# Modulation rows through GpSimd's queue, and every low part of a weight on VectorE, during the state steps

## The chip, the cores and the metric

The kernel runs on one core of a Trainium2 chip. The metric is the time of one execution on the device in microseconds (us); three runs of the kernel before are at hand, and one more execution was profiled.

Names of the engines in the rows: PE is TensorE (PEld its loading of weights), DVE is VectorE, ACT is ScalarE, POOL is GpSimd, SP is SyncE, which here only issues transfers. A name with q at its end (SPq, POOLq) is the engine's sequencer, which waits and issues.

## The reference

One layer of a streaming encoder on 512 frames (`SEQ`) of width D = 2048, in float32: a mixer and a feed-forward part, each between two normalisations. A conditioning vector `c` gives shift, scale and gate for both.

```python
mod = jax.nn.silu(c) @ ada_w + ada_b
...
sh_m, sc_m, g_m, sh_f, sc_f, g_f = jnp.split((mod + ada_table[layer])[:, None, :], N_MOD, axis=-1)
h = _rms(x, norm_mix_pre[layer]) * (1 + sc_m) + sh_m
...
x = x + g_m * _rms(y, norm_mix_post[layer])
h = _rms(x, norm_ffn_pre[layer]) * (1 + sc_f) + sh_f
f = _conv_ffn(h, ffn_w_in[layer], ffn_conv_w[layer], ffn_conv_b[layer], ffn_w_out[layer])
x = x + g_f * _rms(f, norm_ffn_post[layer])
```

The mixer is RWKV-7 with 32 heads of 64. For each head a 64 x 64 state goes through the frames:

```python
sa = jnp.einsum("bhvk,bhk->bhv", state, a_t)
state = (state * w_t[:, :, None, :] + sa[..., None] * b_t[:, :, None, :]
         + v_t[..., None] * k_t[:, :, None, :])
return state, jnp.einsum("bhvk,bhk->bhv", state, r_t)
```

`r`, `k` and `v` are products of the mixed input with 2048 x 2048 weights; the result is normalised per head, gated and multiplied by `w_o`.

## The kernel before

Tiles are 128 channels by 512 frames, so there are KT = 16 blocks of channels (two heads each). Every large product is made in three passes (`mm3`, lines 266 to 273): the 128 x 128 weight and the moving tile are each split into a high part, which is the value rounded to TensorE's faster float32 form, and a low part, the rest; high x high, high x low and low x high are added up in one bank of PSUM.

The weights lie in HBM in the order of their use (`plan`). `w_load` brings a chunk of eight 128 x 128 blocks by SP's queue into one of three buffers `wr`. `w_split` makes the high part `wh` of half a chunk (four blocks, 128 x 512) on ScalarE (line 225) and the low part `wl` by a subtraction (line 227). Which engine subtracts is set by `wst["pool"]`: 0 is VectorE always, 1 is GpSimd always, 2 is GpSimd for every other half. It is 1 in the first stage, 0 from then on, 2 from the start of the state steps (set in `begin`), and 0 again at the output product. Splits run two halves ahead of their use, in four buffers each.

The state is computed in chunks of 64 frames, for two heads at a time, in KT = 16 state steps p = 0 to 15 of eight chunks each. For each step small matrices come through HBM (`d_gs`, `d_bnd`, `d_e`, `d_kp`, `d_vt`), loaded by SP. `inverse(n)` inverts 32 x 32 triangular blocks for four steps at once, in 31 pairs of short GpSimd instructions (lines 715 and 717), after 16 small loads `ia` (line 705), and its result is stored and read back as `tn` and `tt`. `solve(p)` builds a step's matrices (its last products are line 793, which need `tt` as VectorE has filled it in at lines 786 and 787), `transfer` its products (lines 826 and 845), `chain` carries the state on (lines 868 and 876), and `norm` makes the output `y`, which goes by GpSimd's queue to `d_y` (line 908) and comes back by SP as `rl` until there is room for it on the chip. Meanwhile TensorE multiplies the `r` weights, block by block.

All of this is written as generators in a list `sides`; each `mm3` ends with a `tick()`, which moves every generator one yield on, and a few loops tick without a product while something must be waited for. The order of the instructions on each engine is laid out when the kernel is built, by a planner that starts from the order of the program and works with its own costs (`schedule_with_timeline_sim=True`); each engine and each queue then runs its instructions in that order and waits on semaphores.

Shift, scale and gate of the later parts are 64 blocks of 128 values, each a product of 128 rows of `ada_w` with `silu(c)`. `row_jobs` makes them on VectorE: it loads a block of rows to a tile `js`, multiplies it by the row vector `crow` and sums along the row (line 473), and adds the bias (line 474). It has `bufs` buffers, loads the next block some ticks after a block's product, and goes on to the next block after `pace` ticks. `with behind():` puts the product behind the newest low part that VectorE has made. `scan_rows` does 20 of the 64 blocks during the state steps, in two halves of 1024 columns (so 40 loads of 512 KB), with one buffer.

Of the kernel before, what the change touches and what calls it, by code (L numbers as in the profile page):

```python
# [16 lines left out]
P = 128  # L17
# [17 lines left out]
def row_blocks(d):  # L35

    return [(vi, b) for vi in range(2, 6) for b in range(d // P)]
# [122 lines left out]
def body(ctx, tc, g, ap):  # L160
    nc = tc.nc
    KT, FT, GT, D = g.KT, g.FT, g.GT, g.D
    V, S, G, PE = nc.vector, nc.scalar, nc.gpsimd, nc.tensor
# [41 lines left out]
    wst = {"load": 0, "split": 0, "use": 0, "raw": {}, "half": {}, "pool": 0, "end": g.mid}  # L205
# [57 lines left out]
    def behind(on=True):  # L263

        return tc.issue_after(wst["last"].ins) if on else nullcontext()
# [181 lines left out]
    ROWS = row_blocks(D)  # L447
# [4 lines left out]
    def c_row(t, cols=slice(0, D)):  # L452

        n = cols.stop - cols.start
        nc.sync.dma_start(t, d_c.rearrange("k p -> (k p)")[cols].unsqueeze(0).to_broadcast([P, n]))
        return t

    def row_jobs(todo, crow, get, bufs, pace, cols=slice(0, D), lag=0):

        got = {}  # L460

        def load(i):
            if i < len(todo):
                got[i] = get(i % bufs)
                nc.sync.dma_start(got[i], ap["ada3"][ROWS.index(todo[i])][:, cols])

        for i in range(bufs):
            load(i)
        yield
        for n, (vi, b) in enumerate(todo):  # L470
            w, to = got.pop(n), part[:, b:b + 1]
            with behind():
                V.scalar_tensor_tensor(w, w, 1.0, crow, ALU.mult, ALU.mult, accum_out=to)  # L473
            V.tensor_tensor(mods[vi][:, b:b + 1], to, mods[vi][:, b:b + 1] if cols.start else bt[:, vi, b:b + 1], ALU.add)
            for _ in range(lag):
                yield
            load(n + bufs)
            for _ in range(pace - lag):
                yield
# [31 lines left out]
    nc.sync.dma_start(d_c.rearrange("k p -> p k"), cs)  # L511
    crow = c_row(vp.tile([P, D], F32, name="crow"))
    jobs = row_jobs([r for r in ROWS if r[0] == 4], crow, lambda i: vp.tile([P, D], F32, tag="js", name="js", bufs=2), 2, 9)
    vouts = [v_out(vbank[j], j) for j in range(nv0)]
    for o in vouts:
# [54 lines left out]
    def c2(tag, bufs=1, shape=(P, NC, HD)):  # L570
        return pool_of[0].tile(list(shape), F32, tag=tag, name=tag, bufs=bufs)
# [153 lines left out]
    def load_a(p):  # L725
        n, q = p // BP, p % BP
        rhs, ab, tn = (sc.tile([P, NC, n], F32, tag=t, name=t) for t, n in (("rhs", P), ("ab", 32), ("tn", 32)))
        for i, hv in enumerate(HV):
            nc.sync.dma_start(rhs[hv], d_gs[p][hv, :, HD * i:HD * i + P])
            o = 2 * HD * (1 - i)  # L730
            nc.sync.dma_start(ab[i * HD + 32:i * HD + 64], d_gs[p][i * HD + 32:i * HD + 64, :, o:o + 32])
        for h in range(2):
            nc.sync.dma_start(tn[h * HD:h * HD + 32], d_tn[n][q, h, 0].rearrange("c i j -> i c j"))
            for d in range(2):
                o = h * HD + d * 32
                nc.sync.dma_start(TT[o:o + 32, :, o:o + 32], d_tt[n][q, h, d].rearrange("c i j -> i c j"))
        return rhs, ab, tn

    def load_b(p):
        for i, hv in enumerate(HV):  # L740
            nc.sync.dma_start(BH[hv, :, HD - i * HD:P - i * HD], d_bnd[p][hv, :, 2 * i])
        E = sc.tile([P, NC, HD], F32, tag="E", name="E")
        nc.sync.dma_start(E, d_e[p])
        return E

    def load_k(p):
        kp = c2("kp")
        nc.sync.dma_start(kp, d_kp[p])
        return kp

    def load_v(p, h):
        t = svs[h] = c2(f"sv{h}", 1, (P, NC // 2, 2, HD))
        vt = d_vt[p][h * T // 2:(h + 1) * T // 2].rearrange("(c t) (h i) -> h t c i", t=HD, i=HD)
        nc.sync.dma_start(t[HD:P, :, 0], vt[0])
        nc.sync.dma_start(t[0:HD, :, 1], vt[1])
        if h == 0:
            V.memset(t[0:HD, 0, 0], 0.0)
            V.memset(t[HD:P, 0, 1], 0.0)
# [9 lines left out]
    def solve(p):  # L768

        rhs, ab, tn = ld_a.pop(p)  # L770
        up = bank(3, (P, NC, 32))
        us = ab
        for c in range(NC):
            for h in range(2):
                lo = slice(h * HD + 32, h * HD + 64)
                PE.matmul(up[h * HD:h * HD + 32, c], ab[lo, c], TT[lo, c, lo], start=True, stop=True)
        S.copy(us[0:32], up[0:32])
        S.copy(us[64:96], up[64:96])
        for _ in range(2):
            yield  # L780
        wz = bank(3, (P, NC, 32))
        for c in range(NC):
            for h in range(2):
                hi = slice(h * HD, h * HD + 32)
                PE.matmul(wz[hi, c], tn[hi, c], us[hi, c], start=True, stop=True)
        V.tensor_copy(TT[0:32, :, 32:64], wz[0:32])
        V.tensor_copy(TT[64:96, :, 96:128], wz[64:96])
        for _ in range(2):
            yield
        for c0 in (0, 4):  # L790
            hb = bank(4 if c0 else 3, (P, 4, P))
            for c in range(c0, c0 + 4):
                PE.matmul(hb[:, c - c0], TT[:, c], rhs[:, c], start=True, stop=True)  # L793
            cp_ = V.tensor_copy if c0 else S.copy
            cp_(LH[0][HV[1], c0:c0 + 4], hb[HV[1]])
            cp_(LH[1][HV[0], c0:c0 + 4], hb[HV[0]])
            yield
        if p + 1 < KT:
            ld_a[p + 1] = load_a(p + 1)
# [122 lines left out]
    def invert_ready(done):  # L922
        for n in range(NB):
            if n not in begun and done >= (n + 1) * BP:
                begun.add(n)
                sides.append(inv[n])
# [55 lines left out]
    def scan_rows():  # L982
        for cols in (slice(0, D // 2), slice(D // 2, D)):
            row = c_row(c2("crow", 1, (P, D // 2)), cols)
            yield from row_jobs(ROWS[:KT + KT // 4], row, lambda i: c2("js", 1, (P, D // 2)), 1, 8, cols, 2)

    def begin():
        while fixed in sides or inv[0] in sides:
            yield
        ld_a[0], ld_b[0] = load_a(0), load_b(0)  # L990
        for i, hv in enumerate(HV):
            nc.sync.dma_start(LH[i][hv, :, HD - i * HD:P - i * HD], d_bnd[0][hv, :, 2 - 2 * i])
        while s1_last in sides:
            yield
        invert_ready(KT)
        ss_stack.close()
        pool_of[0] = ss_stack.enter_context(tc.tile_pool(name="scn2", bufs=1))
        opened.append(True)
        wst["pool"] = 2
        ld_k[0] = load_k(0)  # L1000
        yield from solve(0)
        load_v(0, 0)
        load_v(0, 1)
        jobs.append(scan_rows())
        sides.extend((s2_a, s2_b, jobs[0]))

    sides.append(begin())
    for b in range(KT):
        ps = bank((kb[KT % 3], kb[(KT - 2) % 3])[b] if b < 2 else 0)
# [141 lines left out]
    for b in range(KT - NL):  # L1151
        if b >= KT - NL - 4:
            fetch_x(*divmod(b - (KT - NL - 4), 2))
        ps = po[b] if b < n0 else kinner("wo", b, yx, bank((2, 6)[b % 2]))
        block_out(b, ps, acc1, yo[b], sqs[b % 2])
        if b == 1:
            jobs = row_jobs(ROWS[KT + KT // 4:2 * KT], c_row(spare("b2", "crow", D)),
                            lambda i: tp.tile([P, D], F32, tag=f"t3{'hl'[i]}", name="js"), 2, 8)
            sides.append(jobs)
# [398 lines left out]
```

## Time and profile before

| | us |
|---|---|
| median of 3 runs | 2728.54 (2727.55 to 2728.64) |
| profiled execution | 2731.33 |
| its span, first to last instruction | 2729.5 |
| TensorE busy | 2573.4 (94%) |
| VectorE busy | 2041.8 (75%) |
| ScalarE busy | 1329.7 (49%) |
| GpSimd busy | 610.8 (22%) |

The profiled execution took 2.8 us more than the median. Busy time of TensorE is modelled, since its products are pipelined: what shows whether it sets the time is where it stands idle and what ended the idle time, and the clock that was granted to it, since at half the clock a product takes twice as long. Idle time of another engine costs nothing by itself.

### The profile page before, as it was taken

Reading aid. Unit: us, or ns where it says so; the run is one execution under the profiler, and the core shown is the slowest. Engines: PE = TensorE matmul, PEld = TensorE weight load, DVE = VectorE, ACT = ScalarE, POOL = GpSimd, SP = SyncE. Lnnn points to the kernel's source line nnn. Section 1 sums busy time; section 2 is a strip of 40 time slices with the busy share of each in tenths; the row PEclk is TensorE's granted clock in tenths of the full one; section 3 lists DMA queues with packets and bytes.
Section 4 is the critical chain, followed back from the end, with each engine's and each line's share of the span. In section 5 each row is a group of like instructions: output and inputs, shape, how many; then the busy total and the mean of one; then the engine's idle time right before and its main releaser. Section 6 shows DMA issues by size and latency. Waiting matters only on the chain.

```text
span 2729.5 us, 46869 instructions
## 1 busy us (share of the span) xinstructions
PE 2573.4 (94%) x17630; PEld 2253.4 (83%) x17630; DVE 2041.8 (75%) x3225; ACT 1329.7 (49%) x2313; POOL 610.8 (22%) x722
## 2 busy tenths in 40 slices
PE   5899999988999998999889999999999999999997
PEld 3568877767778776788789999999999987788896
DVE  6978678887776777667898888888878876544477
ACT  4442355544345445435665555555555553243464
POOL 3543114667531110001422112121121100000000
PEclk8999999999999999999999999999999999999998
DMA  8759876656776666386567767777677658523366
GB/s 304 278 185 388 294 225 209 202 209 208 206 213 179 187 186 169 118 321 219 178 198 205 201 187 198 196 195 204 189 200 197 168 209 287 192 93 101 98 203 205
DMA packets 282419, 559.73 MB, mean 205 GB/s; under 512 B 124016, under 2 KB 157168, under 8 KB 274256
## 3 DMA queue, kind: packets, MB, share of 16 engines
q1 hardware_dynamic: 252400, 445.24, 50.9%
q0 software_dynamic: 29360, 110.77, 15.2%
q8 instruction: 139, 2.28, 0.3%
q14 instruction: 88, 0.72, 0.1%
q10 hardware_dynamic: 432, 0.72, 0.1%
HBM read 478.38 MB, written 78.26 MB: 204 GB/s over the span
## 4 chain that ended last, share of the span: by engine, by line
PE 57%; DMA 10%; DVE 5%; issue 2%; ACT 1%; POOL 1%; SPq 1%; DVEq 0%; ACTq 0%; POOLq 0%
PE bk L1338 10%; PE bk L1336 10%; PE bk L1337 10%; PE bk L270 7%; PE bk L272 7%; PE bk L271 7%; DMA js<-ada 4%; PE bk L845 2%; DMA act<-d_act 1%; DMA tt<-d_tt 1%; PE bk L876 1%; PE bk L793 1%; DVE wl L227 1%; DVE js L473 1%; DMA wr<-w 1%
## 5 line engine op out<-in xcount | busy, mean ns | idle before, releaser
L270 PE MATMUL bk<-xh,wh 128*128 128x512 f32 (+1 forms) x2204 | 781.8, 365 | 23.5 <-ACT wh L225 6.1
L272 PE MATMUL bk<-xh,wl 128*128 128x512 f32 (+1 forms) x2204 | 764.1, 362 | 26.7 <-DVE wl L227 22.6
L271 PE MATMUL bk<-xl,wh 128*128 128x512 f32 (+1 forms) x2204 | 783.9, 360 | 2.1 <-DVE xl L1140 1.7
L225 ACT CAST wh<-wr 128x512 fp32r<-128x512 f32 x584 | 358.0, 620 | 532.9 <-PE bk L271 438.7
L227 DVE TENSOR_TENSOR wl<-wr,wh 128x512 fp32r<-128x512 f32 x518 | 368.9, 717 | 238.3 <-ACT wh L225 221.5
L270 PEld LDWEIGHTS bk<-xh,wh 128*128 128x128 f32 x2204 | 419.7, 192 | 87.9 <-ACT wh L225 7.4
L272 PEld LDWEIGHTS bk<-xh,wl 128*128 128x128 f32 x2204 | 409.4, 191 | 98.8 <-DVE wl L227 33.6
L271 PEld LDWEIGHTS bk<-xl,wh 128*128 128x128 f32 x2204 | 421.3, 192 | 63.1 <-DVE xl L1140 2.7
L1338 PE MATMUL bk<-xh,wl 128*128 128x256 f32 x832 | 235.7, 283 | 0.1
L1336 PE MATMUL bk<-xh,wh 128*128 128x256 f32 x832 | 235.4, 283 | 0.0
L1337 PE MATMUL bk<-xl,wh 128*128 128x256 f32 x832 | 235.4, 283 | 0.0
L1287 POOL DMA_DIRECT2D ss<-w x78 | 68.0, 871 | 623.6 <-DMA ss<-w 385.7
L473 DVE SCALAR_TENSOR_TENSOR js<-js,crow 128x1024 f32<-128x1024 f32 (+1 forms) x100 | 153.8, 1540 | 59.0 <-DMA js<-ada 53.5
L227 POOL TENSOR_TENSOR wl<-wr,wh 128x512 fp32r<-128x512 f32 x66 | 97.7, 1484 | 295.1 <-ACT wh L225 280.1
L1338 PEld LDWEIGHTS bk<-xh,wl 128*128 128x128 f32 x832 | 159.7, 192 | 0.5 <-DVE wl L1323 0.5
L1337 PEld LDWEIGHTS bk<-xl,wh 128*128 128x128 f32 x832 | 159.7, 192 | 0.0
L1336 PEld LDWEIGHTS bk<-xh,wh 128*128 128x128 f32 x832 | 159.7, 192 | 0.0
L1338 PE MATMUL bk<-xh,wx 128*128 128x256 f32 x416 | 117.7, 283 | 0.0
L1336 PE MATMUL bk<-xh,wx 128*128 128x256 f32 x416 | 117.7, 283 | 0.0
L1337 PE MATMUL bk<-xl,wx 128*128 128x256 f32 x416 | 117.7, 283 | 0.0
L1440 POOL TENSOR_TENSOR fo<-fo,rs 128x256 f32<-128x256 f32 x4 | 3.6, 911 | 494.0 <-ACT rs L1102 494.0
L1481 DVE TENSOR_TENSOR xl<-act,xh 128x512 fp32r<-128x512 f32 (+1 forms) x172 | 92.2, 552 | 26.1 <-ACT xh L1480 26.1
(290 smaller groups left out, 5658.2 us busy)
## 6 DMA issues: line engine op xcount, KB each, us to landing
wr<-w SPq DMA_DIRECT2D x370, 512.0 KB
ss<-w SPq DMA_DIRECT2D x78, 512.0 KB
ss<-w POOLq DMA_DIRECT2D x78, 512.0 KB, 8.5
js<-ada SPq DMA_DIRECT2D x72, 512.0 KB
ada<-ada SPq DMA_DIRECT2D x32, 1024.0 KB
js<-ada SPq DMA_DIRECT2D x28, 1024.0 KB
w<-w SPq DMA_DIRECT2D x39, 512.0 KB
d_bnd<-bnd POOLq DMA_DIRECT2D x16, 768.0 KB, 3.7
```

The source lines that it names most:

```text
L225: S.copy(hi, r)
L227: ins = on.tensor_tensor(lo, r, hi.bitcast(F32), ALU.subtract)
L270: PE.matmul(out[:, cs], wh[0:kp, 0:m], xh[0:kp, cs], start=start, stop=False)
L271: PE.matmul(out[:, cs], wh[0:kp, 0:m], xl[0:kp, cs], start=False, stop=False)
L272: PE.matmul(out[:, cs], wl[0:kp, 0:m], xh[0:kp, cs], start=False, stop=stop)
L473: V.scalar_tensor_tensor(w, w, 1.0, crow, ALU.mult, ALU.mult, accum_out=to)
L845: PE.matmul(qb[:, c], LH[i][:, 4 * h + c], RH[i][:, :, 4 * h + c], start=True, stop=True)
L1287: G.dma_start(t[:, i], chunk(j, other), accum_op=ALU.add)
L1336: PE.matmul(ps, wh, xh, start=start and k == 0, stop=False, skip_group_check=True)
L1337: PE.matmul(ps, wh, xl, start=False, stop=False, skip_group_check=True)
L1338: PE.matmul(ps, wl, xh, start=False, stop=k == CH - 1, skip_group_check=True)
L1481: V.tensor_tensor(ahl[e][1][:, cs], act[f][:, cs], ahl[e][0][:, cs].bitcast(F32), ALU.subtract)
```

## The change

The rows of the state steps are loaded by GpSimd's queue (`G` is `nc.gpsimd`) in place of SP's; the other users of `row_jobs` keep SP's. And `wst["pool"]` is no longer set to 2 in `begin`, so it stays 0 and VectorE makes every low part from there on.

```diff
-    def row_jobs(todo, crow, get, bufs, pace, cols=slice(0, D), lag=0):
+    def row_jobs(todo, crow, get, bufs, pace, cols=slice(0, D), lag=0, q=nc.sync):
 
         got = {}
 
         def load(i):
             if i < len(todo):
                 got[i] = get(i % bufs)
-                nc.sync.dma_start(got[i], ap["ada3"][ROWS.index(todo[i])][:, cols])
+                q.dma_start(got[i], ap["ada3"][ROWS.index(todo[i])][:, cols])
...
-            yield from row_jobs(ROWS[:KT + KT // 4], row, lambda i: c2("js", 1, (P, D // 2)), 1, 8, cols, 2)
+            yield from row_jobs(ROWS[:KT + KT // 4], row, lambda i: c2("js", 1, (P, D // 2)), 1, 8, cols, 2, G)
...
         opened.append(True)
-        wst["pool"] = 2
         ld_k[0] = load_k(0)
```

## Rows read from the trace of the kernel before

**Rows 1.** Busy time by stretch: length, then each engine, granted clock, DMA share, GB/s.

```profile
640.00:680.00 40.00, 35.71 (x265) 29.74 (x263) 31.70 (x41) 10.63 (x19) 34.51 (x51) 0.96 0.64 186
680.00:770.00 90.00, 80.80 (x628) 64.95 (x629) 64.84 (x114) 34.81 (x68) 57.19 (x78) 0.92 0.78 208
770.00:1020.00 250.00, 247.95 (x2182) 198.39 (x2181) 179.34 (x347) 120.22 (x233) 32.69 (x30) 1.00 0.71 190
```

**Rows 2.** Instructions of line 227, 680 to 1130 us: minimum, median, maximum in ns.

```profile
L227 DVE TENSOR_TENSOR wl<-wr,wh x34: 673/692/984, 691.0 to 1124.4; 128x512 fp32r<-128x512 f32 x34
...
L227 POOL TENSOR_TENSOR wl<-wr,wh x31: 1257/1277/2279, 692.5 to 1094.3; 128x512 fp32r<-128x512 f32 x31
```

**Rows 3.** List of waits, 680 to 1130 us: in total, times, longest.

```profile
DVE js L473 <- DMA js<-ada: 22.4, 8, 6.8
...
DVE wl L227 <- ACT wh L225: 15.9, 9, 2.6
...
PEld bk L272 <- POOL wl L227: 4.2, 2, 3.8
```

**Rows 4.** Timeline of TensorE's products: start, length, in brackets idle time before.

```profile
725.70 0.79 PE L272 MATMUL bk<-xh,wl 128*128 128x512 f32 x1 [3.41 <-POOL wl L227]
...
734.19 2.05 PE L793 MATMUL bk<-rhs,tt 128*128 128x128 f32 x16
```

**Rows 5.** Busy time by stretch, in the two stretches at half clock.

```profile
725.00:731.80 6.80, 6.10 (x14) 4.79 (x15) 6.35 (x11) 0.62 (x1) 6.41 (x8) 0.50 0.60 174
...
766.00:769.40 3.40, 3.40 (x15) 3.01 (x14) 3.31 (x6) 1.78 (x3) 2.02 (x3) 0.50 0.67 249
```

**Rows 6.** Timeline of GpSimd, the low part that TensorE waited for.

```profile
724.38 1.26 POOL L227 TENSOR_TENSOR wl<-wr,wh 128x512 fp32r<-128x512 f32 x1
```

**Rows 7.** Timeline of VectorE, 708 to 731 us.

```profile
715.22 1.30 DVE L473 SCALAR_TENSOR_TENSOR js<-js,crow 128x1024 f32<-128x1024 f32 x1 [6.77 <-DMA js<-ada]
...
725.23 1.50 DVE L473 SCALAR_TENSOR_TENSOR js<-js,crow 128x1024 f32<-128x1024 f32 x1 [5.20 <-DMA js<-ada]
...
730.40 0.42 DVE L787 COPY tt<-bk 32x256 f32<-32x256 f32 x1
```

**Rows 8.** Timeline of SP's issues, 698 to 748 us.

```profile
698.61 10.90 SPq L705 DMA_DIRECT2D ia<-d_gs x16
...
710.99 0.39 SPq L465 DMA_DIRECT2D js<-ada x1
...
716.56 0.33 SPq L465 DMA_DIRECT2D js<-ada x1
...
747.17 0.56 SPq L465 DMA_DIRECT2D js<-ada x1
```

**Rows 9.** Timeline of VectorE, 741 to 765 us.

```profile
741.03 1.36 DVE L473 SCALAR_TENSOR_TENSOR js<-js,crow 128x1024 f32<-128x1024 f32 x1 [1.30 <-DMA js<-ada]
...
762.92 1.23 DVE L473 SCALAR_TENSOR_TENSOR js<-js,crow 128x1024 f32<-128x1024 f32 x1 [2.79 <-DMA js<-ada]
...
764.49 0.42 DVE L787 COPY tt<-bk 32x256 f32<-32x256 f32 x1
```

**Rows 10.** Timeline of TensorE's products, the stall at 762 us.

```profile
765.01 2.87 PE L793 MATMUL bk<-rhs,tt 128*128 128x128 f32 x16 [2.85 <-issue]
```

**Rows 11.** Instructions of line 227 on GpSimd, 560 to 690 us.

```profile
L227 POOL TENSOR_TENSOR wl<-wr,wh x5: 1265/1402/1745, 636.3 to 675.0; 128x512 fp32r<-128x512 f32 x5
```

**Rows 12.** List of waits of TensorE's products, 636 to 1130 us.

```profile
PE bk L270 <- ACT xh L387: 3.6, 1, 3.6
...
PE bk L686 <- DVE Ab L675: 2.4, 1, 2.4
```

**Rows 13.** Stores of line 908 through GpSimd's queue, 680 to 1130 us.

```profile
L908 POOL DMA_DIRECT2D d_y<-y x14: 540/557/580, 737.0 to 1114.9; - x14
...
DMA to landing us min/median/max: 2.3/4.1/6.0
```

**Rows 14.** Adding loads of line 1287 through GpSimd's queue, 512 KB each.

```profile
DMA to landing us min/median/max: 6.4/8.5/10.4
```

## Prediction

> **What bounds the kernel now.** I read the stage before the engine totals. The state steps lie between about 636 and 1130 us of the span, and the table by stretch [rows 1] is the first view to read there. From 770 to 1020 us TensorE is busy for 247.95 of 250 us and its clock is full; it sets the time, and nothing that VectorE (179.34 busy) or GpSimd (32.69) does there can shorten it. From 680 to 770 it is busy for 80.80 of 90 at a mean clock of 0.92. In that early stretch, and in the short ones at both ends, is all that this change can win or lose directly.
>
> Second, who makes the low parts of the weights (line 227): in 680 to 1130 us VectorE makes 34 at a median of 692 ns, and GpSimd 31 at 1277 ns [rows 2]. Third, the list of waits for the same stretch [rows 3]: TensorE waited for a low part of GpSimd's for 4.2 us in two places, and for none of VectorE's 34. VectorE in its turn stood 22.4 us, eight times, for a row of the modulation (`js`) to land, and 15.9 us for ScalarE's high part in front of its own low parts.
>
> Fourth, the timeline around the longest of these waits. TensorE stands for 3.41 us before the product that takes the low part [rows 4], and the granted clock then is 0.50 (the 1.2 GHz level) from 725.0 to 731.8 us [rows 5]: 6.8 us at half speed, of which TensorE loses 3.4. So this one stall cost 6.8 us. Its low part ran on GpSimd at 724.38 [rows 6], in the middle of the chain of small multiply-adds that inverts the last group of diagonal blocks. VectorE at that time was no better off: it had stood 6.77 us for one row until 715.22, and stood 5.20 us for the next until 725.23; the copy into `tt`, which the product at L793 needs, ended at 730.82 [rows 7]. SP explains the first: it was issuing the 16 small loads of `ia` for 10.90 us from 698.61, so the row's load went out at 710.99; the next went out at 716.56 and landed only after 8.7 us [rows 8].
>
> Fifth, a second stall that rows cause. A `js` load went out at 747.17 [rows 8] although its buffer had been free since 742.39 (741.03 + 1.36 [rows 9]): 4.8 us late on SP. Two products later VectorE stood 2.79 us until 762.92, and the `tt` copies behind that row ended at 764.91 [rows 9]; TensorE, which needs them at L793, stood 2.85 us (the view calls it "issue") until 765.01 [rows 10]. The clock gives way once more for 3.4 us after it [rows 5], 1.7 us lost.
>
> **The change, part by part.** The order of instructions on an engine is laid out when the kernel is built; the trace cannot show the new one, so I leave the old order as it is and move only what the diff moves.
>
> *GpSimd's low parts go to VectorE.* 36 move: the 31 of [rows 2] and five more between 636 and 675 us [rows 11]. GpSimd is rid of the low part that it made late at 724.38. The stall of 3.41 us and the 3.4 us of clock behind it go, if nothing else is late there. What is late next is on VectorE: from 725.70 to L793 at 734.19 [rows 4] are 8.5 us, 3.4 of them lost to the clock, so TensorE, going on at 722.3, would stand at L793 by 727.4, and `tt` would come at 730.82 if the row still lands at 725.23. Then only 734.19 - 730.82 = 3.4 us would be won. But the row loads in front of it can leave earlier: the one of 710.99 waited for SP, and its buffer was free before VectorE fell idle at 708.45 (715.22 - 6.77), 2.5 us before it went out. I take the full **-6.8**, with -3.4 as the other end.
>
> *Their cost on VectorE.* 36 x 0.69 = 24.8 us. In 680 to 1130 it is 31 x 0.69 = 21.4; from 770 to 1020 VectorE has 250 - 179 = 71 us free under a full TensorE, so its share there costs nothing. If that cover were gone it would be 0.69 us per low part. Uncovered are the ends. From 640 to 680 VectorE is busy for 31.70 of 40 [rows 1] and TensorE waits for it (2.4 us for `Ab` [rows 12]): the five are 0 to 3.5 us, taken as **+1**, since the longest of GpSimd's five took 1745 ns against 1265 [rows 11], the two engines were in each other's way, and VectorE gets some of this back. After 1020 us lie 110 of the stretch's 450, so some seven of the 31 if they are evenly spread, among waits of the chain of states: 0 to 5 us, taken as **+1**, for VectorE has free time there too. VectorE also waits in line for ScalarE's high part twice as often; 15.9 us in 34 cases [rows 3] made TensorE wait for no low part, so I charge nothing more.
>
> The row's product (line 473) is put behind the newest low part that VectorE makes, which is now the newest of all; it can only move later, which gives its load more time. Behind it stand `tt`, `qz` and `rh` copies, for which TensorE waits.
>
> *The rows' loads go to GpSimd's queue.* 40 loads of 512 KB leave SP. On SP each took 0.33 to 0.56 us [rows 8] and waited for the row's product; whatever loads stood behind are freed. On GpSimd each stands behind the inversion's steps (57.19 us of work in 78 instructions in 680 to 770, 0.73 us each [rows 1]): about half a step, 0.4 us. While it waits for VectorE's product the inversion waits behind it; that is covered, since the inverted blocks are those of the last four of 16 steps, and the chain is at the first few. Stores of `d_y` wait there too, and are read much later, except at the end. Time to land: on SP 4.2 us (710.99 to 715.22). No load without addition goes by GpSimd's queue in this trace. The nearest rows are the `d_y` stores in these same steps, 256 KB, 2.3 to 6.0 us, median 4.1 [rows 13]; 256 KB more at the stretch's 208 GB/s are 1.3 us, so an estimate of 5.4. The adding loads of 512 KB later in the kernel take 8.5 [rows 14]. I take 5.4, for it is the same queue in the same stretch: 5.4 - 4.2 + 0.4 = 1.6 us more per load. The three loads from 747 to 763 stand in VectorE's way one after another: 3 x 1.6 = 4.8, which is what SP's lateness in front of them gives back. So **0**. The ends: -4.6 if the second stall vanishes (2.85 and the clock's 1.7), and 3 x (8.5 - 4.2 + 0.4) - 4.8 = +9.3 with 8.5 us to land.
>
> *SP's queue is freer.* TensorE waited 3.6 us for a high part of `y` that stood on a fetch through SP near the end of the steps [rows 12]; if the clock fell behind it as behind the first stall, 7.0 in all. The rows are no longer in that queue ahead of it. 0 to -7.0 us; taken as **-1**, since both still share the same transfer engines.
>
> A rule of the Trainium skill speaks against the moved loads. The row: GpSimd's own part of the 14 `d_y` stores took 540 to 580 ns [rows 13], while VectorE was busy for some 72% of the time; it was never held up. The page "SBUF — State Buffer", section "SBUF: two separate sides", states that GpSimd cannot write a DMA's descriptors while VectorE runs an instruction that takes both ports, and that a transfer of about 620 ns then takes about 3100. By the rule each exposed load would be later; by the row, none. The sum goes by the row.
>
> **Sum.** -6.8 + 1 + 1 + 0 - 1 = -5.8 us. The profiled execution took 2731.33 us (span 2729.5), which gives 2725.5; the median of the runs is 2.8 us below it, 2728.54, which gives 2722.7.
>
> **The rivals.** *Stall handed to VectorE (no change).* The low part is made in time, but the rows land as late as now, and TensorE waits for `tt` until 730.82: -3.4 + 1 + 1 - 1 = -2.4, 2726. For it: the row of 725.23 took 8.7 us to land with SP not late at all. Against: SP's 2.5 and 4.8 us of lateness with two others [rows 7 to 9]. Chance 0.30.
>
> *Rows late on GpSimd's queue (slower).* Five loads stand in VectorE's way (those of 715 and 725 us and the three up to 763). With 8.5 us to land each is 4.7 later, 23.5 in all, less SP's 7.3; with -3.4 and +1 for the rest that is +13.8, 2742. It is slower by over 0.2% (5.5 us) from 5x = 5.5 + 3.4 + 7.3 - 1, x = 3.0 us, so from 6.8 us to land. For it: GpSimd works 57 of those 90 us [rows 1]. Against: the 8.5 are of transfers that also read what they add to. Chance 0.20.
>
> *GpSimd held up by VectorE's own instructions (no change).* Each of five exposed loads waits out a row's product, 1.3 to 1.5 us [rows 7]: up to +7.5 on the sum, +1.7, 2730. The 540 to 580 ns speak against it. Chance 0.05. [...]
>
> **How the numbers follow.** Forecast 0.45; the rivals 0.30, 0.20, 0.05. A measurement of this kernel tells about 0.2% (5.5 us) from no change, and the forecast is just beyond. Faster 0.45, same 0.35, slower 0.20. Low end: -6.8 - 4.6 - 7.0 = -18.4, 2710. High end: the slower rival is 2734 at its threshold and 2742 at 8.5 us; I stop at 2740. The forecast's own range is 2710 to 2723.
>
> **What would show it.** No low part on GpSimd after 636 us, 65 on VectorE in the stretch of [rows 2]; no wait of TensorE for a low part; no half clock at 725 to 732; VectorE's wait for rows below 22.4 us, with the first of them, at 715, nearly gone; rows landing in 5 to 6 us; the stretch 770 to 1020 as full as now. I am wrong if TensorE's wait comes back as one for `tt` or `qz` behind a row, if rows take 7 us to land, or if the new order of instructions puts a row's load behind a long part of the inversion.

## The result, and the profile after

The changed kernel takes 2757.4 us (median of four runs, 2752.8 to 2759.84) where the kernel before takes 2728.6: a ratio of 1.0088, 95% interval 1.0068 to 1.0107. It is slower by 0.9%, some 24 us by the ratio and 29 by the medians. The forecast was 2722.7, faster by 5.8 us, with a range that ended at 2740.

The profiled execution took 2758.21 us, 26.9 more than that of before. Busy time by stretch, first of the kernel after (columns as in [rows 1]):

```profile
640.00:680.00 40.00, 35.18 (x255) 30.17 (x254) 33.47 (x45) 10.84 (x20) 36.84 (x52) 0.90 0.62 187
680.00:770.00 90.00, 83.17 (x642) 67.35 (x641) 68.28 (x121) 35.39 (x68) 49.27 (x75) 0.91 0.78 211
770.00:1020.00 250.00, 240.74 (x2029) 190.38 (x2029) 173.53 (x342) 112.11 (x217) 15.51 (x29) 0.97 0.68 176
1020.00:1130.00 110.00, 93.05 (x849) 73.12 (x848) 75.81 (x150) 51.76 (x102) 4.85 (x9) 0.92 0.61 157
1130.00:1420.00 290.00, 265.07 (x1714) 235.38 (x1713) 215.78 (x360) 154.57 (x315) 58.80 (x53) 0.97 0.62 209
```

The two stretches of before that [rows 1] leaves out:

```profile
1020.00:1130.00 110.00, 94.64 (x851) 75.94 (x849) 78.41 (x152) 54.77 (x107) 7.29 (x8) 0.94 0.60 153
1130.00:1420.00 290.00, 267.17 (x1695) 237.42 (x1694) 218.86 (x353) 159.39 (x319) 58.56 (x54) 0.99 0.67 222
```

What TensorE loses in a stretch is its idle time (length less busy) and what the clock takes of the busy time (busy x (1 - clock)). From 680 to 770 us that is 9.2 + 6.5 = 15.7 us before and 6.8 + 7.5 = 14.3 after. From 770 to 1020 it is 2.1 before, and 9.3 + 7.2 = 16.5 after: the stretch that was full is full no longer. With +2.6 (640 to 680), +3.4 (1020 to 1130) and +7.4 (1130 to 1420) the five stretches come to +26.4, nearly all of the 26.9 (an estimate, since the stretches are equal times and not equal work).

The list of waits, 680 to 1130 us, after (in total, times, longest):

```profile
DVE js L473 <- DMA js<-ada: 14.4, 7, 5.3
PE bk L776 <- DMA tt<-d_tt: 10.9, 8, 2.7
PE bk L876 <- DMA sv<-d_vt: 5.6, 5, 2.2
PE bk L826 <- DVE qz L846: 5.4, 2, 3.4
...
PEld bk L272 <- DVE wl L227: 1.1, 1, 1.1
```

and for the same two loads before:

```profile
PE bk L776 <- DMA tt<-d_tt: 5.6, 6, 3.3
...
PE bk L868 <- DMA sv<-d_vt: 1.3, 1, 1.3
PE bk L876 <- DMA sv<-d_vt: 1.1, 1, 1.1
```

VectorE waits less for rows (14.4 us, 22.4 in [rows 3]) and TensorE's wait for a low part is down from 4.2 us to 1.1. What TensorE waits for now are small loads of the state steps on SP's queue: `tt` (32 KB, which `inverse` left in HBM) twice as long, `sv` (64 KB) more than twice; and copies of VectorE's, `qz` above all. The rows land as forecast, here the loads of line 465 through GpSimd's queue (40 of them, ns of issue; the second line is of the landing):

```profile
L465 POOL DMA_DIRECT2D js<-ada x40: 528/528/580, 678.7 to 1168.8; - x40
...
DMA to landing us min/median/max: 4.0/5.6/8.5
```

### The profile page after: what moved, and what is told of

Its sections match the earlier page's. It is cut to its first block, busy times and chain, and to the rows that moved or that the text cites. A ratio compares the mean times of both kernels' runs of the same rounds, so it can differ in the third digit from the quotient of the medians.

```text
span 2756.4 us, 46886 instructions
## 1 busy us (share of the span) xinstructions
PE 2588.9 (94%) x17630; PEld 2264.1 (82%) x17630; DVE 2052.2 (74%) x3261; ACT 1328.4 (48%) x2313; POOL 591.9 (21%) x726
## 4 chain that ended last, share of the span: by engine, by line
PE 60%; DMA 8%; DVE 5%; POOL 2%; issue 2%; SPq 1%; ACT 1%; DVEq 0%; ACTq 0%; POOLq 0%
PE bk L1337 10%; PE bk L1335 10%; PE bk L1336 10%; PE bk L270 8%; PE bk L272 8%; PE bk L271 8%; PE bk L845 2%; DMA wr<-w 1%; DMA js<-ada 1%; PE bk L876 1%; PE bk L793 1%; DVE wl L227 1%; DMA tt<-d_tt 1%; DMA sv<-d_vt 1%; POOL ix L717 1%
## 5 line engine op out<-in xcount | busy, mean ns | idle before, releaser
L227 DVE TENSOR_TENSOR wl<-wr,wh 128x512 fp32r<-128x512 f32 x554 | 392.0, 713 | 255.7 <-ACT wh L225 237.6
L1322 DVE TENSOR_TENSOR wl<-wr,wh 128x512 fp32r<-128x512 f32 x104 | 108.6, 1063 | 3.6 <-ACT wh L1321 1.9
```

The costliest lines, as they stand in the source:

```text
L227: ins = on.tensor_tensor(lo, r, hi.bitcast(F32), ALU.subtract)
L1322: wst["last"] = V.tensor_tensor(lo, r, hi.bitcast(F32), ALU.subtract)
```

## The experiments

Three theories. **A**: the planner lays out a new order of the instructions for the changed kernel, and that order costs the time. **B**: a row load on a queue of its own runs beside the small loads that TensorE waits for; on SP's queue it stood in line with them. **C**: VectorE's added low parts hold up the copies that TensorE waits for.

To part A from the others, a kernel can be held in another's planned order. Both kernels issue the same instructions; only 36 low parts and 40 row loads are on another engine. So each instruction is tied, without a wait, behind the one that stands before it on its engine in the other kernel's plan; the moved ones find their own places:

```python
    for d in zlib.decompress(base64.b85decode("".join(ORDER.split()))).decode().split(","):
        at += int(d)
        i = traced[at]
        if i.engine in last:
            tc.add_manual_dep(i, last[i.engine], info, reason="order")
        last[i.engine] = i.name
```

In the traces, every run held so has its instructions on each engine in the order of the kernel whose plan it was given, low parts and row loads left out. The ties by themselves cost nothing that shows: `new_order_first` below, which is held throughout, stands at 1.0004.

"Old order" is the plan of the kernel before, "new order" that of the kernel after. The runs of before spread more here than in the first four (2718 to 2742 us), so ratios to the runs of before on the same chip are given.

**Both changes in the old order, and neither in the new.** `after_in_old_order` is the kernel after with the loop above and before's plan; `before_in_new_order` the reverse.

> The kernel after (rows by GpSimd's queue, all low parts on VectorE), but every instruction that both kernels have on the same engine is held in the planned order of the kernel before, on each engine; only the 36 low parts and the 40 row loads find their own places. Theory A (the planner's new order of the instructions costs the 29 us): 2722 to 2731 us, not slower than before. Theory B (row loads on a queue of their own run beside the small loads of the state steps and make them land late): 2750 to 2760. Theory C (VectorE's 24.8 us of added low parts hold up the copies that TensorE waits for): 2745 to 2760.

Measured: 2742.0 us, 1.0038 (1.0016 to 1.0059).

> The kernel before (rows by SP's queue, every other low part on GpSimd), with every instruction that both kernels have on the same engine held in the planned order of the kernel after. Theory A (order): 2750 to 2760 us. Theories B (row loads beside small loads) and C (VectorE's added work): 2726 to 2732, as before.

Measured: 2744.3 us, 1.0062 (1.0038 to 1.0085). Neither time lies in the range of a theory, and none of the three stands alone: the order by itself costs some 17 us, and the two changes by themselves, in the old order, some 10.

**One change alone, each in its own plan.**

```diff
+        wst["pool"] = 2
```

in `begin` of the kernel after makes `rows_only`; taking `G` out of the call of `row_jobs` makes `lows_only`.

> Only the row loads go to GpSimd's queue; GpSimd still makes every other low part. Theory B (row loads beside the small loads): 2750 to 2760 us. Theory C (VectorE's added work): 2726 to 2731, as before. Theory A (order): about as before too, 2725 to 2735, since the planned order differs little from that of the kernel before.

Measured: 2751.0 us, 1.0080 (1.0057 to 1.0103).

> Only the low parts go to VectorE; the rows stay on SP's queue. Theory B (row loads beside the small loads): 2722 to 2729 us, the stall at 722 us gone and nothing lost. Theory C (VectorE's added work): 2750 to 2760. Theory A (order): 2745 to 2760, since here the planned order moves as far from that of before as in the kernel after.

Measured: 2731.9 us, 1.0017 (1.0000 to 1.0033). The rows carry the loss, but each kernel has a plan of its own here (by the traces that of `rows_only` too departs from the old order, which was not expected), so the sizes mix with A. The next runs hold the order.

**One change alone, in a fixed order.** The same two edits, in the old order, and the low parts alone also in the new.

> Only the row loads go to GpSimd's queue, and every other instruction is held in the planned order of the kernel before. Theory B (the row loads' own queue): the whole loss that the two moves made in the old order, 10 to 14 us, is here: 2738 to 2744 us, and more where a low part of GpSimd's stands behind a row load that waits. Theory C (VectorE's added work): 2726 to 2731.

Measured: 2744.1 us, 1.0043 (1.0026 to 1.0060).

> Only the low parts go to VectorE, and every other instruction is held in the planned order of the kernel before. Theory B (the row loads' own queue): 2720 to 2730 us, the low part of 722 us no longer late and nothing lost. Theory C (VectorE's added work): 2738 to 2744.

Measured: 2735.1 us, 1.0015 (1.0001 to 1.0029).

> The kernel after with its rows put back on SP's queue, every other instruction held in the planned order of the kernel after. Theory B (the row loads' own queue): 2738 to 2748 us, what that order costs with rows and low parts as before. Theory C (VectorE's added work): 2750 to 2760, as after.

Measured: 2743.1 us, 1.0051 (1.0032 to 1.0070). In the old order the rows cost 0.43% and the low parts 0.15%. In the new order the low parts add nothing to the order's 0.62% (0.51% with them), and moving the rows to GpSimd's queue takes 0.51% to 0.88%. So the rows' own queue costs some 0.4% in either order by these two pairs; by a third pair, both changes in the old order (0.38%) less the low parts alone (0.15%), it is 0.2%. Each of these differences is sure only to some 0.2 to 0.3%. C is hardly told from nothing: with the rows moved as well, the old order is no slower for the low parts (0.38% against 0.43%).

The old order with VectorE's low parts shows why they gain nothing. Timeline of TensorE's products in `lows_in_old_order` (idle time before in brackets):

```profile
730.60 2.02 PE L793 MATMUL bk<-rhs,tt 128*128 128x128 f32 x16 [1.20 <-issue]
...
742.80 0.33 PE L876 MATMUL bk<-qz,sv 128*64 128x64 f32 x2 [2.07 <-DVE sv L872]
...
766.37 3.04 PE L793 MATMUL bk<-rhs,tt 128*128 128x128 f32 x16 [3.23 <-issue]
...
1039.63 0.50 PE L272 MATMUL bk<-xh,wl 128*128 128x512 f32 x1 [4.05 <-DVE wl L227]
```

and of VectorE ahead of the last of them:

```profile
1035.56 1.39 DVE L829 TENSOR_TENSOR rh<-bk,cst 64x512 f32<-64x512 f32 x2
1036.88 1.38 DVE L815 TENSOR_TENSOR ri<-rsb,E 64x512 f32<-64x512 f32 x2
1038.27 0.58 DVE L872 TENSOR_SCALAR sv<-bk,el 64x64 f32<-64x64 f32 x2
1038.88 0.69 DVE L227 TENSOR_TENSOR wl<-wr,wh 128x512 fp32r<-128x512 f32 x1
```

The stall of [rows 4] is gone, and TensorE comes to L793 at 730.60 (734.19 in [rows 4]), after 1.20 us (again called "issue") for the `tt` copies, which end at 730.50. Part of that is given back at once: TensorE stands 2.07 us at 742 for a copy of VectorE's, which had waited for a row until 740.49, then as long as before at L793 (3.23, 2.85 in [rows 10]), and later 4.05 us for a low part that VectorE reaches behind the three other lines shown.

**What the row loads do on their own queue.** `lows_in_new_order` and the kernel after have the same order on every engine and differ in the rows' queue alone. First the waits in 680 to 1130 us, then the middle stretch by busy time, with the rows on SP's queue:

```profile
DVE js L473 <- DMA js<-ada: 14.4, 7, 3.8
PE bk L776 <- DMA tt<-d_tt: 6.5, 6, 2.2
...
PE bk L270 <- ACT xh L387: 5.2, 1, 5.2
...
PE bk L876 <- DMA sv<-d_vt: 3.9, 4, 2.4
```

```profile
770.00:1020.00 250.00, 245.48 (x2138) 194.70 (x2136) 181.87 (x361) 117.30 (x228) 4.87 (x9) 0.99 0.69 187
```

VectorE waits 14.4 us for rows in both, so in all the rows keep it waiting no longer. `tt` is 6.5 against 10.9, `sv` 3.9 against 5.6. From 770 to 1020 us, where the loss (idle time and clock, as above) is 7.0 us here and 16.5 in the kernel after, TensorE waits 2.3 us for `tt` here and 6.7 there, and over 0.8 us in all for nothing else. One and the same step, with the rows on SP's queue (SP's issues, then the product that needs `tt`):

```profile
883.49 2.51 SPq L736 DMA_DIRECT2D tt<-d_tt  x4
886.10 1.19 SPq L741 DMA_DIRECT2D bh<-d_bnd  x2
887.38 0.56 SPq L465 DMA_DIRECT2D js<-ada  x1
888.04 0.38 SPq L212 DMA_DIRECT2D wr<-w  x1
...
888.67 0.24 PE L776 MATMUL bk<-tt,ab 32*32 32x32 f32 x2
```

and in the kernel after (SP, GpSimd, TensorE; then the stretch behind it by busy time):

```profile
893.54 2.09 SPq L736 DMA_DIRECT2D tt<-d_tt  x4
895.72 1.19 SPq L741 DMA_DIRECT2D bh<-d_bnd  x2
...
894.67 0.53 POOL L465 DMA_DIRECT2D js<-ada  x1 [15.46 <-DVE js L473]
...
899.97 0.21 PE L776 MATMUL bk<-tt,ab 32*32 32x32 f32 x2 [2.12 <-DMA tt<-d_tt]
```

```profile
900.80:911.00 10.20, 10.20 (x81) 7.28 (x80) 5.38 (x13) 1.58 (x5) 0.53 (x1) 0.50 0.40 120
```

On SP's queue the row goes out behind the four `tt` loads and the two `bh`, and the product runs 5.2 us after the first `tt` without a wait. On GpSimd's queue nothing holds the row but its own product, so it leaves in the middle of the `tt` loads: these are there 6.4 us after the first, TensorE stands 2.12 us, and the granted clock is 0.50 (1.2 GHz) for the next 10.2, some 5.1 us more by an estimate (half of the 10.2); with the rows on SP's queue it is 1.00 from 888 to 899. A second place shows less: a row goes out at 827.66, just ahead of the `tt` loads of 828.49, TensorE stands 2.65 us for them until 836.84, and 3.4 us at half clock follow; but in the same step with the rows on SP's queue it stands 1.16 us for them too (until 828.93), and 3.5 us at a clock of 0.52 follow.

**The bytes.** `rows_short` is the kernel after, held in its own order. The main lines of its edit (the row's product is also taken times zero, and both halves share one `js` tile):

```diff
-                q.dma_start(got[i], ap["ada3"][ROWS.index(todo[i])][:, cols])
+                n = 128 if q is G and (i or cols.start) else cols.stop - cols.start
+                q.dma_start(got[i][:, :n], ap["ada3"][ROWS.index(todo[i])][:, cols.start:cols.start + n])
...
```

> The kernel after in its own planned order, but a row load brings 128 of its 1024 columns (64 KB in place of 512; only the first is whole), and the row's product is taken times zero, so that the modulation of the later parts is its bias alone. Theory B by the bytes (row transfers hold up the small loads beside them): 2735 to 2747 us. Theory B by the queue alone, whatever the size, or theory C (VectorE's added work): 2750 to 2760.

Measured: 2732.4 us, 1.0013 (0.9998 to 1.0027), below the range of either theory. Its waits and its middle stretch (line numbers behind the edit are one higher):

```profile
DVE js L474 <- DMA js<-ada: 5.8, 3, 3.5
PE bk L777 <- DMA tt<-d_tt: 4.8, 6, 2.3
```

```profile
770.00:1020.00 250.00, 247.95 (x2162) 197.24 (x2162) 183.90 (x365) 120.56 (x235) 16.70 (x31) 1.00 0.56 147
```

As many loads on the same queue, with VectorE's work and the order unchanged, and the stretch is full again, with 1.2 us of waiting for `tt` in it: it is the bytes. `rows_short_before` is the same edit in the kernel before, rows on SP's queue.

> The kernel before in its own planned order, rows on SP's queue, but a row load brings 128 of its 1024 columns (only the first is whole), and the row's product is taken times zero, so that the modulation of the later parts is its bias alone. If row transfers hold up the small loads only where they run beside them on another queue (theory B): 2725 to 2730 us, as before. If the bytes cost the same wherever they are queued: 2705 to 2715.

Measured: 2718.5 us, 0.9954 (0.9937 to 0.9972), between the two ranges. Two waits and the stretch from 680 to 770 us:

```profile
PE bk L777 <- DMA tt<-d_tt: 4.2, 4, 3.1
...
DVE js L474 <- DMA js<-ada: 3.8, 4, 2.4
```

```profile
680.00:770.00 90.00, 86.48 (x700) 69.88 (x700) 73.81 (x130) 38.52 (x75) 61.72 (x76) 0.96 0.68 166
```

So row bytes are not free on SP's queue either: seven eighths of them cost 0.46% there, and 0.75% (1.0088 less 1.0013) on GpSimd's. The difference of 0.3% is no larger than the two intervals leave open, so this pair alone does not tell the queues apart; the runs in a fixed order do. Nor is the 0.46% mainly a matter of the small loads: `tt` goes from 5.6 us to 4.2, while VectorE's wait for rows goes from 22.4 to 3.8. From 680 to 770 us, where TensorE waited for no `tt` in the kernel before, 7.0 us are lost in place of 15.7; the second stall behind a late row [rows 10] is gone, and the wait for the high part of `y` [rows 12] is 1.8 us in place of 3.6. On SP's queue the bytes cost by making the rows late, and what stands behind them; that they also hold up the small loads ahead of them is not shown. The new order's cost shows once more, as far as the pair can tell it: with short rows the new order stands at 1.0013 and the old at 0.9954, 0.6% apart, but the low parts and the queue differ too.

**Another queue beside SP's.** `rows_on_act` puts `S` in place of `G` in the call, new order.

> The kernel after with its rows on ScalarE's queue, every other instruction held in the planned order of the kernel after. If any queue beside SP's does the harm, by letting a row pass the small loads: 2752 to 2770 us (ScalarE's copies also stand behind a row load that waits for its buffer). If it is GpSimd's queue itself: 2738 to 2748, as with the rows on SP's in that order.

Measured: 2753.4 us, 1.0088 (1.0066 to 1.0110); TensorE waits 9.1 us for `tt`. As with GpSimd's queue. ScalarE's copies behind a waiting row load may be a part of it, so this run agrees with B but does not prove that any second queue does it.

**An attempt to disturb the plan.** `lag3` is the kernel before with `cols, 3` for `cols, 2` in the call of `row_jobs`.

> The kernel before with each row load put one tick later in the program (lag 3 for 2), queues and engines unchanged; the planner lays out a new order. Theory A (a new order by itself costs some 15 us, as the kernel before in the new order did): anything from 2715 to 2745 us, outside 2724 to 2733. Otherwise 2726 to 2731.

Measured: 2728.9 us, 0.9991 (0.9977 to 1.0005). This run does not bear on A: by line and tile, the instructions and loads of its trace follow one another on every engine exactly as in the kernel before, so there was no new order to test, and it is the kernel before once more. That a new plan need not cost time is seen in `lows_only`: against the kernel before, 407 of VectorE's 2503 instructions (low parts left out) stand at another place in its trace, 352 in that of the kernel after, and it takes 1.0017, its low parts included.

**Smaller row loads.** `rows_quarter`, the kernel before with

```diff
-        for cols in (slice(0, D // 2), slice(D // 2, D)):
-            row = c_row(c2("crow", 1, (P, D // 2)), cols)
+        for q in range(4):
+            cols = slice(q * D // 4, (q + 1) * D // 4)
+            row = c_row(c2("crow", 1, (P, D // 4)), cols)
```

and `js` of D // 4 columns, pace 4, lag 1.

> The kernel before with the rows in four passes of 512 columns in place of two of 1024: twice as many row loads on SP's queue, of 256 KB each, at twice the rate. Theory B (a small load waits for the row transfer that it stands behind or beside): 2715 to 2727 us, less the planner's new order. If only the bytes in all count, or the order: 2728 to 2745.

Measured: 2740.6 us, 1.0037 (1.0023 to 1.0052). Slower: from 680 to 1130 us VectorE now waits 78.0 us, 42 times, for rows (22.4 us, 8 times in [rows 3]). A likely reason is that half the bytes do not land in half the time: issued at 815.01 and 824.56 us, two of these rows are there at 817.98 and 827.91, 3.0 and 3.4 us, where one of 512 KB took 4.2 and another 8.7 [rows 7, 8], and one issued at 809.13 in the kernel before 4.0. The hope that smaller pieces would spare the small loads is not borne out; what this plan costs by itself was not parted from it.

**Where the new order costs its time.** The kernel before, with the new order in one part of the program only.

> The kernel before, its engines and queues unchanged, with the new order of instructions only up to about 880 us (the first half of the state steps), the old order behind it. If the order's cost of about 16 us lies here: 2740 to 2747 us. If it lies in the places where the copies of the last state step come late in the new order (1104 to 1135 us), as I expect: 2724 to 2731, since the profile in the new order had lost nothing yet by 900 us.

Measured: 2731.4 us, 1.0004 (0.9993 to 1.0014).

> The kernel before with the new order only from about 880 to 1180 us (the second half of the state steps). If the order's cost lies in the late copies of the last state steps: 2736 to 2746 us. If it is in the first half or spread: 2729 to 2735.

Measured: 2740.4 us, 1.0034 (1.0021 to 1.0046).

> The kernel before with the new order only after about 1180 us, where the stretch 1130 to 1420 lost 13 us more than before in the profile of the new order. If those 13 us are the order's: 2738 to 2745 us. If they are the chance of one execution: 2728 to 2732, for only 142 instructions of TensorE are moved there.

Measured: 2734.6 us, 1.0019 (1.0008 to 1.0031), between the two ranges. The three add up to 0.57%, the whole order to 0.62%: nothing before 880 us, over half of it between 880 and 1180, the rest after. Waits of TensorE's products from 880 to 1180 us in `new_order_second`:

```profile
PE bk L270 <- ACT xh L387: 5.9, 1, 5.9
PE bk L793 <- DVE qz L846: 2.6, 2, 2.4
PE bk L776 <- DMA tt<-d_tt: 2.4, 2, 2.1
PE bk L876 <- DVE sv L872: 2.0, 3, 1.4
PE bk L876 <- DMA sv<-d_vt: 2.0, 4, 0.7
PE bk L845 <- DVE qz L846: 1.6, 2, 1.0
PE bk L826 <- ACT lh L796: 1.3, 2, 0.9
PE bk L270 <- DVE rh L829: 1.2, 1, 1.2
```

and in the kernel before:

```profile
PE bk L776 <- DMA tt<-d_tt: 5.0, 5, 3.3
PE bk L270 <- ACT xh L387: 3.6, 1, 3.6
PE bk L270 <- DVE mod L474: 1.9, 1, 1.9
PE bk L270 <- ACT wh L225: 1.2, 1, 1.2
PE bk L876 <- DMA sv<-d_vt: 1.1, 1, 1.1
```

The new order has products stand closer behind the copies that feed them: `qz`, `sv`, `rh` and `lh`, none of them over 0.6 us before, together cost 8.7 us (2.6 + 2.0 + 1.6 + 1.3 + 1.2), and `xh` 5.9 in place of 3.6, while `tt` costs 2.6 less and the waits for `mod` and `wh` (1.9 and 1.2) are gone. In all TensorE is busy for 277.68 of these 300 us, 283.20 before, and its mean clock is 0.96, 0.98 before. I expected the late copies of the last state step (1104 to 1135 us) to be all of it; they are a part.

## Why the prediction was wrong

**"I leave the old order as it is and move only what the diff moves."** This is the step that failed first and, by the medians, by most: the order the planner lays out for the changed kernel costs 0.62% by itself, some 17 us, with every engine and queue as before. The prediction named the new order only in its last sentence, as something that would prove it wrong, and gave it neither a price nor a chance.

**"So 0", for the rows on GpSimd's queue.** The parts that were priced were right: 5.6 us to land against an estimate of 5.4, issue in 528 to 580 ns, and VectorE's wait for rows down to 14.4 us. The price was looked for in the wrong place. It counted how late the row is for VectorE, and not how late the row makes others. The loads that it runs beside are for TensorE, and cost 0.4%, 10 to 12 us. "SP's queue is freer", taken as -1, came true in its own place: TensorE's wait for the high part of `y` (`xh`), 3.6 us in [rows 12] and 5.2 with the rows on SP's queue in the new order, is gone in the kernel after, and in the old order with the rows alone moved. What it left out is that on SP's queue the small loads had gone out ahead of the rows. In the Trainium skill, the page "DMA: Bandwidth & Descriptors", section "Queues, rings and completion order", says that a DMA engine takes one queue's requests in order and alternates, packet by packet, between the queues that have work. The trace agrees in its effect (first `tt` issue to product 6.4 us beside a row, 5.2 us ahead of it), but no run here shows the packets. The rule was there to be weighed, and the prediction weighed another.

**"From 770 to 1020 us ... nothing that VectorE or GpSimd does there can shorten it."** True, but the prediction went on as if nothing could lengthen it either. For VectorE's low parts that held: with them alone, in the old order, the stretch is busy for 248.32 of 250 us at full clock. In the kernel after it loses 16.5 us, with the same order and the rows on SP's queue 7.0, and with short rows 2.1: most of what broke it is the rows' transfers.

**-6.8 for GpSimd's late low part.** In the old order, the one for which it was worked out, the stall does go, but the time is not won: 1.0015 where -6.8 + 1 + 1 would be 0.9982. The rival "stall handed to VectorE" is what the timeline shows at first (L793 reached at 730.60, where it said 730.82), but its -2.4 was not won either: 2.07 us go at 742, and 4.05 at 1039 in a stretch priced at +1. And in the new order the low part is hardly late even on GpSimd: `before_in_new_order` waits 1.2 us for one there (3.41 in [rows 4]), and has 84.53 us busy from 680 to 770. So what looks in the profile after like the forecast gain (1.1 us of waiting for low parts in place of 4.2) cannot be credited to the move: the order by itself does as much.

**The rival "rows late on GpSimd's queue"** had the sign right, the place only in part, and the mechanism wrong: it needed 6.8 us to land for five loads up to 763 us, and the loss came at 5.6 us, with 4.9 us of it from 680 to 770 (9.4 lost with the rows on SP's queue in the same order, 14.3 after) and 9.5 from 770 to 1020. GpSimd held up by VectorE did not appear: 40 loads were issued in 528 to 580 ns each, with VectorE busy for 173.5 of 250 us in the middle stretch. Which of VectorE's instructions there take both ports no row shows, so these times do not test the rule as such.

The sum of what was found: order +0.62%, low parts -0.11% (in the new order; not told from nothing), rows +0.37%, together the 0.88% measured. It adds up by construction, for each part is the difference of two kernels on the way from before to after, and each is sure only to some 0.2 to 0.3%. What stays open is how the rows' queue costs 4.9 us from 680 to 770, how much of ScalarE's queue's loss is the second queue, and which single displaced instruction costs how much after 880 us.

## What to carry to other kernels

Price a moved bulk load by what it will run beside, and look first for the small loads that the busiest engine waits for: in line behind them it waits its turn, on a queue of its own it does not. Where a planner lays out the instructions, a change of engines is also a change of order, which here cost 0.62%, against some 0.4% for the rows' queue; hold the order fixed before believing what a change is worth, and see in the trace that an order meant to differ does differ. A stall that is removed is a gain only if the next thing in line is early: ask what the engine that takes over the work will make late.

## What the runs showed of the hardware

On a queue beside that of the small loads, taking away seven eighths of the bytes of the 512 KB row loads gave 0.75%, and TensorE's wait for the small `tt` loads went from 10.9 us to 4.8; on the small loads' own queue it gave 0.46%, and that wait went only from 5.6 to 4.2. A transfer of half the size did not land in half the time: 3.0 and 3.4 us for two loads of 256 KB, 4.2 and 4.0 for two of 512, and one of 512 took 8.7; these few were read, not all. And the clock adds to the price of a short wait: after 2.12 us of idle time at 897 us TensorE ran at 1.2 GHz for 10.2 us, which by an estimate (half of them) cost 5.1 more.
